# A two-pass matmul encoder layer: other offsets for the MLP's split weights, and another order of products in half of its first layer

## The chip, the cores and the metric

The kernel runs on one core of one Trainium2 chip. The metric is the device time of the program in microseconds (us); lower is better. Names of engines: PE is TensorE (PEld its weight loads), DVE is VectorE, ACT is ScalarE, POOL is GpSimd, SP is SyncE, which issues the DMAs.

## The reference, cut to what matters

One layer of an encoder over 256 tokens of width 2048, in float32: a mixer (retention and a gated delta rule), a cross-attention, a squared-ReLU MLP with hidden width 8192, and a last RMSNorm. The change touches the MLP alone:

```python
h = rms_norm(x, norm_ffn_g[l])
x = x + jnp.square(jax.nn.relu(h @ w_ff1[l])) @ w_ff2[l]
return rms_norm(x, norm_final_g)
```

`w_ff1` is 2048 by 8192 and `w_ff2` 8192 by 2048, so each holds 64 MB.

## The kernel before, in words

Every large product is made of three products of rounded parts. A float32 operand is split into a high part (rounded to the matmul type `float32r`) and a low part (the rest): high times high, high times low and low times high are added up in PSUM. The activations are held already split in tiles called `q` ("quads"): 4 blocks of 128 features, each with 256 columns of high and then 256 columns of low part.

`fetch` (L74) brings 1 MB of weights: one DMA into a tile `raw` (3 buffers), and then two halves, each split by ACT (`whi`, L92: a copy that rounds) and by DVE (`wlo`, L93: `raw` minus `whi`). `whi` and `wlo` have 3 buffers of 4096 bytes per partition each in the pool `wpipe`. `fetch` runs at a high priority of the scheduler, which orders each engine's instructions at build time by a model of their times and of what they depend on; on the chip each engine then follows its own list.

Two helpers use these halves:

- `blocks` (L155) computes 256 output features as two PSUM tiles `s0` and `s1` (b = 0 and 1). The weights are the stationary operand (128x128), the activations the moving one. For each of the 16 blocks of the inner dimension and each b it issues L171, a high product (stationary `whi`, 512 moving columns: both parts of the activations), and L172, a low product (stationary `wlo`, 256 moving columns: the high part). A call has 32 such pairs. Layer one of the MLP is 32 calls (fb = 0 to 3, b2 = 0 to 7, L936); the projections before it are made in the same way.
- `chunk` (L119) computes 512 output features with the activations stationary and the weights moving: L133 (`whi`), L134 (`wlo`) and L135 (`whi` again), 512 columns each. A call has 96 such matmuls. Layer two of the MLP is 16 calls (fb, n; L985), the last of them with `hold`, which keeps its splits in `q` tiles.

All `whi`, `wlo` and `q` tiles that MLP products read begin at a multiple of 512 bytes in a partition, and so does each slice of them: every stationary or moving operand of the MLP has offset 0 modulo 512 bytes. Three pads in the code (56 floats at L58, `PAD1`, `PAD2`) put the pools there. The delta rule's `kh` and `kl` lie at 96 modulo 512, and the retention's `vh`, `vl`, `sth` and `stl` at 288.

Ahead of the MLP stands the output projection of the cross-attention, `residual_pass` (L820) with `w_xo`. For each block of its output ACT copies half of the PSUM tile (`bo`, L176), DVE adds the other half (L177) and the residual (`rt`, L831), ACT scales and rounds it into the next `q` (L834) and squares it (L837), DVE makes the low part (L835) and adds the square to `acc2` (L838). Behind the last block PE sums `acc2` over partitions (L843). The tiles `acc2`, `sq2` and those of the attention are in the pool `xattn`, which is closed at L909. The pool `mlp` (`gfin`, `res`, `hs`) is opened behind it, at the same address. PE also transposes `rt` into `res` there (L920, 32 transposes, copied by ACT at L921).

Of the kernel before, what the change touches and what calls it, by code (L numbers as in the profile page):

```python
# [11 lines left out]
F32R = mybir.dt.float32r  # L12
# [5 lines left out]
P = 128  # L18
D = 2048
S = 256  # L20
NT = S // P
KT = D // P
# [8 lines left out]
THETA = 10000.0  # L31

PAD1, PAD2 = 8, 80
TWO_PI = 2.0 * math.pi
BIG = 1.0e30

# [13 lines left out]
def trunk(ctx: ExitStack, tc: tile.TileContext, x, mem, positions, norm_mix_g, w_in, conv_w, gdn_a_log, gdn_dt_bias,  # L50
# [4 lines left out]
    act, vec, pool, pe = nc.scalar, nc.vector, nc.gpsimd, nc.tensor  # L55
# [15 lines left out]
        return psp.tile([P, 512], F32, name="b", tag="b", bufs=4)  # L71


    def fetch(pieces, k, n, rush=False, hold=None):  # L74

        raw = wp.tile([P, k * n], F32, name="raw", tag="raw", bufs=3)
        rv = raw.rearrange("p (k n) -> p k n", k=k)
        with tc.high_priority(offset=100000):
            for off, ap in pieces:
                src = ap.rearrange("(k p) n -> p k n", p=P)  # L80
                for ks in ((slice(0, k // 2), slice(k // 2, k)) if rush else (slice(0, k),)):
                    nc.sync.dma_start(rv[:, ks, off:off + ap.shape[1]], src[:, ks, :])
            got = []
            for i in range(2):
                if hold:
                    both = hold().both
                    hi, lo = (both[:, a:a + 2, :].rearrange("p a s -> p (a s)") for a in (0, 2))
                else:
                    hi = wp.tile([P, k * n // 2], F32R, name="whi", tag="whi", bufs=3)
                    lo = wp.tile([P, k * n // 2], F32R, name="wlo", tag="wlo", bufs=3)  # L90
                src = raw[:, i * k * n // 2:(i + 1) * k * n // 2]
                act.activation(hi, src, AF.Copy)  # L92
                vec.tensor_sub(lo, src, hi.bitcast(F32))  # L93
                got.append((hi.rearrange("p (k n) -> p k n", n=n), lo.rearrange("p (k n) -> p k n", n=n)))
        return got
# [20 lines left out]
    def quad_a():  # L116
        return new_quad(hqp, 5)

    def chunk(quads, pieces_of, evac, before=None, hold=None):  # L119


        ps = stream_ps()
        parts = [(t, 0, 512, ps[t]) for t in range(NT)]
        if hold:
            parts[1:] = [(1, 0, 256, ps[1][:, :256]), (1, 256, 512, bank()[:, :256])]
        held = {q: fetch(pieces_of(q), 4, 512, hold=hold) for q in ((2, 3) if hold else ())}

        def products(q, i, part, halves):
            t, c0, c1, o = part
            xh, xl = (a[:, i, t * P:(t + 1) * P] for a in quads[q])  # L130
            wh, wl = (a[:, i % 2, c0:c1] for a in halves[i // 2])
            first, last = q == 0 and i == 0, q == 3 and i == 3
            pe.matmul(o, xh, wh, start=first, stop=False)  # L133
            pe.matmul(o, xh, wl, start=False, stop=False)  # L134
            pe.matmul(o, xl, wh, start=False, stop=last)  # L135

        for q in range(4):
            if q not in held:
                if before:
                    before(q)  # L140
                halves = fetch(pieces_of(q), 4, 512, rush=before is not None and q == 0)
# [10 lines left out]
    def cols(w, c0, n=512):  # L152
        return lambda q: [(0, w[q * 512:(q + 1) * 512, c0:c0 + n])]

    def blocks(quads, w, c0, nb, evac):  # L155

        k = 16 // nb
        ps = stream_ps()  # L160
        n = nb * P
        for g in range(KT // k):
            halves = fetch([(0, w[g * k * P:(g + 1) * k * P, c0:c0 + n])], k, n)
            for i in range(k):
                kk = g * k + i
                xh, xhl = quads[kk // 4][0][:, kk % 4, :], quads[kk // 4].both[:, kk % 4, :]
                wh, wl = halves[i // (k // 2)]
                for b in range(nb):
                    bs = slice(b * P, (b + 1) * P)
                    lh, ll = wh[:, i % (k // 2), bs], wl[:, i % (k // 2), bs]  # L170
                    pe.matmul(ps[b], lh, xhl, start=kk == 0, stop=False)  # L171
                    pe.matmul(ps[b][:, :S], ll, xh, start=False, stop=kk == KT - 1)  # L172
        for b in range(nb):
            with tc.high_priority(offset=50000):
                o = sm.tile([P, S], F32, name="bo", tag="bo", bufs=2)
                act.activation(o, ps[b][:, S:], AF.Copy)  # L176
                vec.tensor_add(o, o, ps[b][:, :S])  # L177
                evac(b, o)
# [131 lines left out]
    for k2 in range(8):  # L310
        ps = bank()
# [598 lines left out]


    fp = ctx.enter_context(tc.tile_pool(name="mlp", bufs=2))
    gfin = fp.tile([P, D], F32, name="gfin", tag="gfin", bufs=1)
    nc.sync.dma_start(gfin, norm_final_g.partition_broadcast(P))
    res = fp.tile([P, NT, D], F32, name="res", tag="res", bufs=1)
# [7 lines left out]
    for fb in range(4):  # L923
        hid = []
        for b2 in range(8):
            hs = fp.tile([P, 2, S], F32, name="hs", tag="hs", bufs=2)
            if b2 % 2 == 0:
                hid.append(quad_a())

            def evac_h(b, ps):  # L930
                vec.scalar_tensor_tensor(hs[:, b, :], ps, 0.0, ps, op0=ALU.max, op1=ALU.mult)  # L931
                qh, ql = (a[:, b2 % 2 * 2 + b, :] for a in hid[-1])
                act.activation(qh, hs[:, b, :], AF.Copy)  # L933
                vec.tensor_sub(ql, hs[:, b, :], qh.bitcast(F32))  # L934

            blocks(h3, w_ff1[0], fb * D + b2 * 256, 2, evac_h)  # L936
        for n in range(4):
            ns = slice(n * 512, (n + 1) * 512)

            def add(t, ps, c0, c1):  # L940
                got = res[:, t, n * 512 + c0:n * 512 + c1]
                vec.scalar_tensor_tensor(got, ps, rstd3q[:, t:t + 1], got, op0=ALU.mult, op1=ALU.add)  # L942
                return got

            def evac_o(t, ps, c0, c1):
                got = add(t, ps, 0, 512)
                if fb == 3:
                    square_sum(ssq4[:, t, n:n + 1], got)
                    vec.tensor_mul(got, got, gfin[:, ns])

            def evac_last(t, ps, c0, c1):
                got = add(t, ps, c0, c1)
                acc = ssq4[:, t, 4 if c0 else 3:5 if c0 else 4]
                if t == 0:
                    square_sum(acc, got)
                else:
                    junk = sm.tile([P, 512], F32, name="junk", tag="junk", bufs=1)
                    vec.scalar_tensor_tensor(junk[:, :256], got, 1.0, got, op0=ALU.mult, op1=ALU.mult, accum_out=acc)
                if not c0:
                    s = sm.tile([P, 1], F32, name="s4", tag="s4")  # L960
                    vec.tensor_reduce(s, ssq4[:, t, 0:4], axis=AX.X, op=ALU.add)
                    vec.tensor_scalar(s, s, 1.0 / D, EPS, op0=ALU.mult, op1=ALU.add)
                    sums.append(s)
                else:
                    vec.scalar_tensor_tensor(sums[t], acc, 1.0 / D, sums[t], op0=ALU.mult, op1=ALU.add)
                if c1 < 512:
                    return
                r = sm.tile([P, 1], F32, name="r4", tag="r4")
                rsqrt(r, sums[t])
                if t == 0:  # L970
# [12 lines left out]
            last = fb == 3 and n == 3  # L983
            sums = []
            chunk(hid, cols(w_ff2[0, fb * D:(fb + 1) * D, :], n * 512), evac_last if last else evac_o,  # L985
                  hold=quad_b if last else None)


_INS = ["x", "mem", "positions", "norm_mix_g", "w_in", "conv_w", "gdn_a_log", "gdn_dt_bias", "ret_gn_g", "gdn_norm_g",
# [24 lines left out]
```

## Time and profile before

| what | us |
|---|---|
| device time, median of 3 runs | 2132.74 (2132.52 to 2136.52) |
| span of the profiled execution, first to last instruction | 2135.2 |
| PE busy, share of the span | 2102.0, 98% |
| DVE busy, share | 1411.1, 66% |
| ACT busy, share | 1094.2, 51% |
| stage of the MLP in the span | about 1416 to the end |

The profile gives one time for its execution, the span; it lies 2.5 us above the median and inside the three runs. A matmul's busy time in the profile is longer than the distance to the next one, since matmuls are pipelined and their ends are modelled: what one costs in a stream is read from the distances of the starts, or from how many of them a stretch of time holds. The granted TensorE clock (PEclk) is 1.00 in the whole MLP but its last few us.

### The profile page before, as it was taken

What the parts mean: (1) busy time and instruction counts of PE and PEld (TensorE: products, weight loads), DVE (VectorE), ACT (ScalarE), POOL (GpSimd) and SP (SyncE); (2) the same over time, 40 slices, a digit from 0 to 9 for tenths busy, and PEclk for the clock granted to TensorE, in tenths of its full rate; (3) what the DMA queues carried; (4) which work ended last, traced back from release to release, by engine and by line L of the source; (5) the groups of instructions that cost most, each with busy time, mean ns of one, the idle gap of its engine ahead of it and who ended that gap; (6) DMA issues with size and microseconds to landing.
All of it is one profiled execution on the core that took longest, in us unless ns stands there. A gap on an engine that the chain in (4) does not pass through costs nothing.

```text
span 2135.2 us, 28778 instructions
## 1 busy us (share of the span) xinstructions
PE 2102.0 (98%) x11172; PEld 1800.1 (84%) x11172; DVE 1411.1 (66%) x2225; ACT 1094.2 (51%) x1700; POOL 28.5 (1%) x39
## 2 busy tenths in 40 slices
PE   8999999799999999999999999999999999999998
PEld 6878888688888889888888888888888888888887
DVE  5765779578667866786557666766556555645655
ACT  7565565354556455645455555554434434434444
POOL 0000000000000000000000000000000000000000
PEclk9999999999999999999999999999999999999999
DMA  8777656355545654555457654565566556556653
GB/s 293 249 243 241 197 183 198 96 186 194 176 144 197 202 182 144 171 199 192 156 172 256 197 187 148 178 198 180 194 197 184 192 196 185 190 197 185 189 197 138
DMA packets 316009, 405.91 MB, mean 190 GB/s; under 512 B 16592, under 2 KB 224480, under 8 KB 315744
## 3 DMA queue, kind: packets, MB, share of 16 engines
q1 hardware_dynamic: 315872, 404.08, 58.3%
q8 instruction: 87, 1.43, 0.3%
q14 instruction: 50, 0.41, 0.1%
HBM read 390.40 MB, written 13.65 MB: 189 GB/s over the span
## 4 chain that ended last, share of the span: by engine, by line
PE 93%; DMA 3%; ACT 1%; DVE 1%; SPq 1%; issue 0%; POOL 0%; ACTq 0%; POOLq 0%; DVEq 0%
PE s L171 33%; PE s L172 16%; PE s L134 13%; PE s L135 13%; PE s L133 13%; PE b L650 2%; DMA dec_d<-dec_w 1%; DMA xc<-x 1%; PE b L561 0%; DMA ct<-scr_t 0%; PE b L103 0%; DVE wlo L93 0%; PE b L104 0%; PE b L105 0%; DMA row<-crow 0%
## 5 line engine op out<-in xcount | busy, mean ns | idle before, releaser
L93 DVE TENSOR_TENSOR wlo<-raw,whi 128x1024 fp32r<-128x1024 f32 x702 | 858.4, 1224 | 521.4 <-ACT whi L92 515.4
L92 ACT ACTIVATE whi<-raw 128x1024 fp32r<-128x1024 f32 x702 | 743.9, 1061 | 727.3 <-PE s L135 377.1
L171 PE MATMUL s<-q,whi 128*128 128x512 f32 x3088 | 1080.7, 398 | 1.2 <-DVE bo L177 0.9
L172 PE MATMUL s<-q,wlo 128*128 128x256 f32 x3088 | 844.3, 281 | 5.9 <-DVE wlo L93 5.8
L171 PEld LDWEIGHTS s<-q,whi 128*128 128x128 f32 x3088 | 572.5, 188 | 126.1 <-DVE bo L177 1.2
L172 PEld LDWEIGHTS s<-q,wlo 128*128 128x128 f32 x3088 | 583.2, 189 | 20.7 <-DVE wlo L93 8.8
L134 PE MATMUL s<-wlo,q 128*128 128x512 f32 x1264 | 494.0, 391 | 0.8 <-DVE wlo L93 0.8
L135 PE MATMUL s<-whi,q 128*128 128x512 f32 x1264 | 491.3, 390 | 0.0
L133 PE MATMUL s<-whi,q 128*128 128x512 f32 x1264 | 449.5, 391 | 0.3 <-ACT whi L92 0.3
L134 PEld LDWEIGHTS s<-wlo,q 128*128 128x128 f32 x1264 | 237.8, 188 | 49.9 <-DVE wlo L93 2.0
L133 PEld LDWEIGHTS s<-whi,q 128*128 128x128 f32 x1264 | 237.3, 188 | 50.1 <-ACT whi L92 0.7
L135 PEld LDWEIGHTS s<-whi,q 128*128 128x128 f32 x1264 | 237.6, 188 | 48.2
L176 ACT ACTIVATE bo<-s 128x256 f32<-128x256 f32 x193 | 73.2, 379 | 129.5 <-PE s L172 116.8
L177 DVE TENSOR_TENSOR bo<-bo,s 128x256 f32<-128x256 f32 x193 | 80.4, 417 | 49.9 <-ACT bo L176 49.9
L516 DVE SCALAR_TENSOR_TENSOR acc<-bo,cw,acc 128x255 f32<-128x255 f32 (+2 forms) x144 | 66.1, 478 | 2.0 <-ACT acc L513 1.0
L616 DVE TENSOR_TENSOR pr<-lw,tw 32x31 f32<-32x31 f32 (+15 forms) x124 | 40.4, 325 | 9.8 <-DMA lw<-scr_l 7.7
L618 DVE TENSOR_TENSOR tw<-tw,pr 32x31 f32<-32x31 f32 (+15 forms) x124 | 40.7, 328 | 2.6
L942 DVE SCALAR_TENSOR_TENSOR res<-s,rstd3q,res 128x512 f32<-128x512 f32 (+1 forms) x32 | 22.3, 736 | 12.0 <-PE s L135 12.0
L751 ACT ACTIVATE gth<-s 128x512 f32<-128x512 f32 x32 | 19.0, 593 | 17.9 <-PE s L135 15.5
L931 DVE SCALAR_TENSOR_TENSOR hs<-bo 128x256 f32<-128x256 f32 x64 | 27.1, 423 | 1.1
L934 DVE TENSOR_TENSOR q<-hs,q 128x256 fp32r<-128x256 f32 x64 | 26.8, 419 | 0.9 <-ACT q L933 0.9
L933 ACT ACTIVATE q<-hs 128x256 fp32r<-128x256 f32 x64 | 26.2, 410 | 0.0
(292 smaller groups left out, 1084.5 us busy)
## 6 DMA issues: line engine op xcount, KB each, us to landing
raw<-w_in SPq DMA_DIRECT2D x144, 1024.0 KB, 4.9
raw<-w_ff SPq DMA_DIRECT2D x128, 1024.0 KB, 5.3
raw<-w_xkv SPq DMA_DIRECT2D x31, 1024.0 KB, 6.2
raw<-w_out SPq DMA_DIRECT2D x16, 1024.0 KB, 6.2
raw<-w_xq SPq DMA_DIRECT2D x16, 1024.0 KB, 6.1
raw<-w_xo SPq DMA_DIRECT2D x16, 1024.0 KB, 5.1
dec_d<-dec_w SPq DMA_DIRECT2D x16, 192.0 KB, 4.7
dec<-dec_d SPq DMA_DIRECT2D x8, 384.0 KB, 3.2
```

Of the source, the lines that this page charges most:

```text
L92: act.activation(hi, src, AF.Copy)
L93: vec.tensor_sub(lo, src, hi.bitcast(F32))
L133: pe.matmul(o, xh, wh, start=first, stop=False)
L134: pe.matmul(o, xh, wl, start=False, stop=False)
L135: pe.matmul(o, xl, wh, start=False, stop=last)
L171: pe.matmul(ps[b], lh, xhl, start=kk == 0, stop=False)
L172: pe.matmul(ps[b][:, :S], ll, xh, start=False, stop=kk == KT - 1)
L176: act.activation(o, ps[b][:, S:], AF.Copy)
L177: vec.tensor_add(o, o, ps[b][:, :S])
L516: vec.scalar_tensor_tensor(acc[:, d:], ps[:, :S - d], cw[:, j, blk:blk + 1], acc[:, d:], op0=ALU.mult, op1=ALU.add)
L618: vec.tensor_sub(tw[:, j + 1:32, 0:j + 1], tw[:, j + 1:32, 0:j + 1], pv)
L650: pe.matmul(pv[:, i, :], lhs(i), rhs[:, i, :], start=True, stop=True)
```

## The change

In the MLP alone the split halves of `fetch` come from a new pool, `mweights`, opened with the pool `mlp`. Its tiles, `mhi` and `mlo`, are 128 floats longer than `whi` and `wlo`, 4608 bytes, which is 9 times 512, and each begins at a multiple of 512 bytes; there are 3 buffers of each. A call uses a slice of them that begins 8 a floats into the tile, with a number `a` from 0 to 15 for the high part and 5 a modulo 16 for the low part; `a` counts the calls of a layer. So each call has its own pair of offsets, multiples of 32 bytes; within a call they stay. The first call of each layer, and call 16 of layer one, have (0, 0). The last call of layer two keeps `wpipe` and `q`, as before.

In layer one, for fb = 2 and 3 (16 of the 32 calls), the order within a block of the inner dimension becomes high b=0, high b=1, low b=0, low b=1, instead of high, low, high, low.

The pool `mweights` lies at bytes 190976 to 218624 of a partition; `xattn`, closed just ahead, had 162304 to 211560, so the two overlap. Where a new pool lies over a closed one, its first tiles wait for the last instruction that used the closed pool.

```diff
+PLACE = 128
...
-    def fetch(pieces, k, n, rush=False, hold=None):
+    def fetch(pieces, k, n, rush=False, hold=None, place=None):
...
+                elif place:
+                    own, at = place
+                    hi, lo = (own.tile([P, k * n // 2 + PLACE], F32R, name=e, tag=e, bufs=3)[:, a:a + k * n // 2]
+                              for e, a in zip(("mhi", "mlo"), at))
                 else:
...
-                for b in range(nb):
-                    bs = slice(b * P, (b + 1) * P)
-                    lh, ll = wh[:, i % (k // 2), bs], wl[:, i % (k // 2), bs]
-                    pe.matmul(ps[b], lh, xhl, start=kk == 0, stop=False)
-                    pe.matmul(ps[b][:, :S], ll, xh, start=False, stop=kk == KT - 1)
+
+                def high(b):
+                    pe.matmul(ps[b], wh[:, i % (k // 2), b * P:(b + 1) * P], xhl, start=kk == 0, stop=False)
+
+                def low(b):
+                    pe.matmul(ps[b][:, :S], wl[:, i % (k // 2), b * P:(b + 1) * P], xh, start=False, stop=kk == KT - 1)
+
+                if turns:
+                    for part in (high, low):
+                        for b in range(nb):
+                            part(b)
+                else:
+                    for b in range(nb):
+                        high(b)
+                        low(b)
...
+    mwp = ctx.enter_context(tc.tile_pool(name="mweights", bufs=3))
...
-            blocks(h3, w_ff1[0], fb * D + b2 * 256, 2, evac_h)
+            u = fb * 8 + b2
+            blocks(h3, w_ff1[0], fb * D + b2 * 256, 2, evac_h, place=(mwp, (8 * (u % 16), 8 * (5 * u % 16))), turns=fb > 1)
...
-                  hold=quad_b if last else None)
+                  hold=quad_b if last else None, place=None if last else (mwp, (8 * (4 * fb + n), 8 * (5 * (4 * fb + n) % 16))))
```

What this does to the lists of the engines: up to the end of the `w_xo` projection they stay as they were, and the differences begin there. ACT's list at that place, before, with the semaphores that an instruction waits for in brackets (`whi_13202` is the first split of `w_ff1`, `bo_13122` the copy of the last block of `w_xo`):

```order
L92 ACTIVATE whi_13202<-raw_13200 128x1024 [waits DMAHW2_49,PE_49,Activation_49]
L92 ACTIVATE whi_13206<-raw_13200 128x1024 [waits PE_49,Activation_49]
L176 ACTIVATE bo_13113<-s0_13027 128x256 [waits PE_49]
L92 ACTIVATE whi_13244<-raw_13242 128x1024 [waits DMAHW3_49,DVE_49,PE_49]
L176 ACTIVATE bo_13122<-s1_13028 128x256 [waits PE_49]
L834 ACTIVATE q_12922<-rt_10298,gains_84 128x256 [waits DVE_49]
L837 ACTIVATE sq2_13119<-rt_10298 128x256
```

ACT's list at the same place, with the change (`mhi_13205` is now the first split of `w_ff1`; L97, L191, L849 and L852 are L92, L176, L834 and L837 of before):

```order
L191 ACTIVATE bo_13113<-s0_13027 128x256 [waits PE_49]
L191 ACTIVATE bo_13122<-s1_13028 128x256 [waits PE_49]
L849 ACTIVATE q_12922<-rt_10298,gains_84 128x256 [waits DVE_49]
L852 ACTIVATE sq2_13119<-rt_10298 128x256 [waits Activation_49]
L849 ACTIVATE q_12922<-rt_10298,gains_84 128x256 [waits DVE_49]
L852 ACTIVATE sq2_13128<-rt_10298 128x256 [waits Activation_49]
L97 ACTIVATE mhi_13205<-raw_13203 128x1024 [waits DMAHW2_49,DVE_49,PE_49]
```

The first splits of the MLP stood ahead of the last work of `w_xo`; now the first stands behind all of it. The values that it waits for on DVE and PE are those of the last add to `acc2` (L838) and of the second sum over `acc2` (L843). PE's list at that place, before (`s1_13028` is the last block of `w_xo`, `s0_13198` the first of `w_ff1`):

```order
L171 MATMUL s1_13028<-q_12262,whi_13077 128x512
L172 MATMUL s1_13028<-q_12262,wlo_13078 128x256
L171 MATMUL s0_13198<-q_12295,whi_13202 128x512
L172 MATMUL s0_13198<-q_12295,wlo_13203 128x256
L171 MATMUL s1_13199<-q_12295,whi_13202 128x512
```

PE's list there with the change (L858 is the sum of L843, L936 the transposes of L920; L175 and L178 are the high and the low product):

```order
L175 MATMUL s1_13028<-q_12262,whi_13077 128x512
L178 MATMUL s1_13028<-q_12262,wlo_13078 128x256
L858 MATMUL b_13131<-ones_77,acc2_12293 128x2 x2
L936 MATMUL b_13150<-ident_76,rt_10298 128x128 x4
L936 MATMUL b_13156<-ident_76,rt_10298 128x128 x4
L936 MATMUL b_13162<-ident_76,rt_10298 128x128 x4
L936 MATMUL b_13168<-ident_76,rt_10298 128x128 x4
L175 MATMUL s0_13201<-q_12295,mhi_13205 128x512
L175 MATMUL s1_13202<-q_12295,mhi_13205 128x512
L178 MATMUL s0_13201<-q_12295,mlo_13206 128x256
```

Before, the first product of layer one followed the last of `w_xo` at once; now the sum and 16 of the 32 transposes stand between them. The other change of order is in layer one from fb = 2 on. PE's list at the start of that part, before (`s0_16507` and `s1_16508` are b = 0 and 1):

```order
L171 MATMUL s0_16507<-q_12295,whi_16511 128x512
L172 MATMUL s0_16507<-q_12295,wlo_16512 128x256
L171 MATMUL s1_16508<-q_12295,whi_16511 128x512
L172 MATMUL s1_16508<-q_12295,wlo_16512 128x256
L171 MATMUL s0_16507<-q_12295,whi_16511 128x512
```

The same place with the change:

```order
L175 MATMUL s0_16510<-q_12295,mhi_16514 128x512
L175 MATMUL s1_16511<-q_12295,mhi_16514 128x512
L178 MATMUL s0_16510<-q_12295,mlo_16515 128x256
L178 MATMUL s1_16511<-q_12295,mlo_16515 128x256
L175 MATMUL s0_16510<-q_12295,mhi_16514 128x512
```

The same five products stand there, the two high ones now ahead of the two low ones. On SP the load of `gfin` (1 MB) has moved ahead of one `w_ff1` load.

More of the change, by code (lines that the diff above doesn't have):

```diff
@@ L117, in quad_a, with chunk @@
         return new_quad(hqp, 5)
-    def chunk(quads, pieces_of, evac, before=None, hold=None):
+    def chunk(quads, pieces_of, evac, before=None, hold=None, place=None):
         ps = stream_ps()
@@ L140, in chunk @@
                     before(q)
-                halves = fetch(pieces_of(q), 4, 512, rush=before is not None and q == 0)
+                halves = fetch(pieces_of(q), 4, 512, rush=before is not None and q == 0, place=place)
                 for i in range(4):
@@ L153, in cols, with blocks @@
         return lambda q: [(0, w[q * 512:(q + 1) * 512, c0:c0 + n])]
-    def blocks(quads, w, c0, nb, evac):
+    def blocks(quads, w, c0, nb, evac, place=None, turns=False):
         k = 16 // nb
@@ L162, in blocks @@
         for g in range(KT // k):
-            halves = fetch([(0, w[g * k * P:(g + 1) * k * P, c0:c0 + n])], k, n)
+            halves = fetch([(0, w[g * k * P:(g + 1) * k * P, c0:c0 + n])], k, n, place=place)
             for i in range(k):
```

## The prediction

> **What bounds the kernel now.** I read the page first: the busy times, then the chain that ended last.
>
> ```profile
> PE 2102.0 (98%) x11172; PEld 1800.1 (84%) x11172; DVE 1411.1 (66%) x2225; ACT 1094.2 (51%) x1700; POOL 28.5 (1%) x39
> PE 93%; DMA 3%; ACT 1%; DVE 1%; SPq 1%; issue 0%; POOL 0%; ACTq 0%; POOLq 0%; DVEq 0%
> ```
>
> PE carries 93% of the chain, so time is won or lost only where PE's products get closer or further apart, or where PE stands still. Next I read two stretches inside the MLP, the first of layer two and the second of layer one.
>
> ```profile
> core 0: us, PE busy (x) PEld busy (x) DVE busy (x) ACT busy (x) POOL busy (x), PEclk, DMA share, GB/s
> 1510.00:1590.00 80.00, 80.00 (x355) 66.24 (x354) 41.75 (x42) 32.40 (x33) 0.00 (x0) 1.00 0.58 196
> 1600.00:1680.00 80.00, 80.00 (x459) 69.69 (x459) 50.27 (x70) 38.34 (x57) 0.00 (x0) 1.00 0.62 190
> ```
>
> PE is busy all 80 us at clock 1.00, DVE and ACT at most 63%. Each count holds two products begun before the stretch. So layer one starts 457 products in 80 us, 175 ns apiece, 350 ns for a pair of high and low; layer two 353, 226.6 ns apiece. No stall is left in there: in the MLP the change can act only on these two spacings, and at the seam where the MLP begins.
>
> **The seam.** This is the one part that the lists of the engines fix. PE, ACT and DVE now, at the end of `w_xo`:
>
> ```profile
> 1415.82 0.27 PE L172 MATMUL s<-q,wlo 128*128 128x256 f32 x1
> 1415.93 0.40 PE L171 MATMUL s<-q,whi 128*128 128x512 f32 x1
> ...
> 1425.36 0.50 PE L843 MATMUL b<-ones,acc 128*128 128x2 f32 x4
> ...
> 1430.12 1.91 PE L920 MATMUL b<-ident,rt 128*128 128x128 f32 x16
> ```
>
> ```profile
> 1415.79 0.39 ACT L176 ACTIVATE bo<-s 128x256 f32<-128x256 f32 x1 [1.42 <-PE s L172]
> 1416.07 1.05 ACT L92 ACTIVATE whi<-raw 128x1024 fp32r<-128x1024 f32 x1
> 1417.02 0.38 ACT L176 ACTIVATE bo<-s 128x256 f32<-128x256 f32 x1
> 1417.29 0.51 ACT L834 ACTIVATE q<-rt,gains 128x256 fp32r<-128x256 f32 x1
> 1417.69 0.41 ACT L837 ACTIVATE sq<-rt 128x256 f32<-128x256 f32 x1
> ```
>
> ```profile
> 1416.21 0.42 DVE L177 TENSOR_TENSOR bo<-bo,s 128x256 f32<-128x256 f32 x1 [0.58 <-ACT bo L176]
> 1416.67 0.42 DVE L831 TENSOR_TENSOR rt<-bo,rt 128x256 f32<-128x256 f32 x1
> 1417.16 1.23 DVE L93 TENSOR_TENSOR wlo<-raw,whi 128x1024 fp32r<-128x1024 f32 x1
> 1418.30 0.42 DVE L177 TENSOR_TENSOR bo<-bo,s 128x256 f32<-128x256 f32 x1
> 1418.63 0.48 DVE L835 SCALAR_TENSOR_TENSOR q<-rt,gains,q 128x256 fp32r<-128x256 f32 x1
> ...
> 1421.10 0.48 DVE L835 SCALAR_TENSOR_TENSOR q<-rt,gains,q 128x256 fp32r<-128x256 f32 x1
> 1421.49 0.42 DVE L838 TENSOR_TENSOR acc<-acc,sq 128x256 f32<-128x256 f32 x1
> ```
>
> Today the last low product of `w_xo` starts at 1415.82 and the first of `w_ff1` 0.11 us later, since its splits were made ahead; PE gets to the sum L843 only at 1425.36, when `acc2` has long been done. With the change no split of `w_ff1` may be written before that sum has read `acc2`, so all of it lies bare. By the rows: the last low product ends at 1416.10. ACT's second `bo` follows at 1416.1, no longer behind a 1.05 us split (today 1417.02). DVE then has two L177 and two L831; such instructions follow each other at 0.33 us (1418.30 to 1418.63), so the second L831 ends at 1417.6. ACT's two L834 and two L837 follow each other at 0.4 us (1417.29 to 1417.69), the last ending at 1418.9, and DVE's L835 and L838 (0.39 apart) end at 1419.4. PE's sum starts at 1419.45, where the next product stood at 1415.93: 3.5 us lost. The sum ends at 1419.95; the first `mhi` takes 1.05, to 1421.0, the first `mlo` 1.23 more, to 1422.3. PE meanwhile does sum and 16 transposes, work that it has today later (so no loss), to 1421.5, then two high products of 0.23, and waits about 0.4 us for `mlo`. Together **+3.9 us**, and I hold 3.0 to 4.5 possible: not below, as nothing else is on PE's list there. Queued behind the waiting split on ACT are only other splits and the copies of `res`; on DVE `rstd3q`, which waits 0.8 us for POOL inside the same hole. The load of `gfin`, now ahead of a `w_ff1` load on SP, costs nothing: three loads have landed by then, 17 us of products at 350 ns a pair, against a landing time of 5.3 us for 1 MB.
>
> A hole of that length has a second price. The trace has one like it, a wait for `wlo` early on, and the stretch that follows:
>
> ```profile
> 163.10:165.70 2.60, 0.03 (x1) 0.00 (x0) 1.61 (x3) 1.10 (x5) 0.00 (x0) 1.00 0.58 217
> ...
> 166.20:169.60 3.40, 3.40 (x13) 2.88 (x12) 1.91 (x2) 2.72 (x8) 0.00 (x0) 0.51 0.72 185
> ```
>
> After 2.6 us without products the clock was granted at 0.51 for 3.4 us, which loses 3.4 x 0.49 = 1.7 us. I take **+1.7 us**; 0 if the drop does not come or falls on the transposes alone, 3.3 for two such stretches. The Trainium skill, "TensorE: Matmul & The Clock Gate", Part 1, says the clock is set by free-running windows of 3413 ns and halves after an idle one; the 3.4 us at 0.51 agree, and by that rule a hole just over a window long either contains one or doesn't: 1.7 or nothing.
>
> **The offsets.** No row shows MLP products at another offset than 0, nor a stationary and a moving operand at different offsets. The nearest rows have both away from 0: the delta rule's `kh`, `kl` at 96 modulo 512, the retention's `vh`, `sth` at 288, beside the attention's at 0. All rows are means of one shape.
>
> ```profile
> L103 PE MATMUL b<-kth,qth 128*128 128x256 f32 x32 | 9.0, 282 | 0.0
> ...
> L561 PE MATMUL b<-kl,kh 128*128 128x512 f32 x16 | 6.3, 395 | 0.0
> ...
> L103 PE MATMUL b<-vh,sth 128*128 128x256 f32 x24 | 6.1, 281 | 0.0
> ```
>
> And layer two, at 0, from the stretch 1510 to 1590:
>
> ```profile
> L133 PE MATMUL s<-whi,q 128*128 128x512 f32 x118 | 41.2, 389 | 0.0
> ```
>
> With 256 columns offset makes no difference (281 and 282 ns). With 512 it is 395 against 389, 6 ns more. But these runs are three products long, and a layer-two run at offset 0 also starts slowly after a wait:
>
> ```profile
> 31.43 0.39 PE L135 MATMUL s<-whi,q 128*128 128x512 f32 x1
> ...
> 32.58 0.39 PE L135 MATMUL s<-whi,q 128*128 128x512 f32 x1
> ```
>
> Five products in 1.15 us there, 230 ns, before they settle at 226.6. So PE falls into step after a few products; part of the 6 ns is such a start. *Layer two:* 14 calls have new offsets, 14 x 96 = 1344 products; at 6 ns 8.1 us, at 0 nothing. High and low weights now alternate between two offsets as moving operand, which should keep PE out of step part of the time: I take half, **+4.0 us**. *Layer one:* the weights are stationary, the rest stays at 0, and slower and quicker pairs stand beside each other today already, 0.36 us (1612.73 to 1613.09, below) and 0.35. I take **0**, from the 256-column rows; the bounds are every pair at 0.36 us, 10 ns over the mean, in 30 calls of 32 pairs, +9.6 us, and the gain in the first rival.
>
> **The order.** In fb = 2 and 3, 16 calls have 16 quads of high, high, low, low, 256 in all. The list of before has such a quad here and there:
>
> ```profile
> 1612.73 0.40 PE L171 MATMUL s<-q,whi 128*128 128x512 f32 x1
> ...
> 1613.09 0.40 PE L171 MATMUL s<-q,whi 128*128 128x512 f32 x1
> ...
> 1613.44 0.63 PE L171 MATMUL s<-q,whi 128*128 128x512 f32 x2
> 1613.91 0.39 PE L172 MATMUL s<-q,wlo 128*128 128x256 f32 x2
> 1614.13 0.40 PE L171 MATMUL s<-q,whi 128*128 128x512 f32 x1
> ...
> 1614.83 0.40 PE L171 MATMUL s<-q,whi 128*128 128x512 f32 x1
> ```
>
> The quad takes 0.69 us (1613.44 to 1614.13), the two pairs behind it 0.70 (to 1614.83): at most 2.6 us over 256 quads, at the rows' rounding. I take half, **-1.3 us**, between -2.6 and +1.
>
> **The sum.** 3.9 + 1.7 + 4.0 + 0 - 1.3 = +8.3 us. On the profiled execution that gives 2135.2 + 8.3 = 2143.5; the runs' median is 2.5 lower, and the forecast is made from it: 2132.74 + 8.3 = **2141.0 us**, +0.4%. Splits as such cost nothing: the same 1024 elements per instruction on DVE and ACT, both at most 63% busy under PE.
>
> **Rivals.** *First, the other side: faster.* If stationary and moving operand at one offset are in each other's way, the 226.6 ns hold a wait that other offsets take away. For it: the 16 transposes take 1.91 us, so with some 0.27 off for the length of the last they start (1.91 - 0.27)/15 = 109 ns apart with a full weight load each, so (an estimate) 218 ns would do for 512 columns and 327 for a pair. Against: `kh` and `kl` away from 0 were not quicker. All of it would be 1344 x 9 + 960 x 23 ns = 34 us; half of it -17, with the seam and the order -13: about 2120. It wins from 2.6 ns saved per product on (8.6 us by 1344 + 1920 products; seam and order together then come to -4.3).
>
> *Second, offsets do nothing*, because PE falls into step as before: 3.9 + 1.7 - 1.3 = +4.3, 2137.0, the edge between same and slower. The Trainium skill's "SBUF — State Buffer", Who interferes with whom, says that TensorE has separate read ports for the two operands and never waits on anyone: by that rule it is this rival. The 281 and 282 ns agree, the 395 against 389 does not.
>
> *Third, every product pays.* Layer two at 6 ns (+8.1), layer one at 360 ns a pair (+9.6), with the seam's 5.6: +23.3 us, 2156. For it: a step once lost is lost for whole calls, since the offsets last a call. Against: the 256-column rows.
>
> That the change doesn't do what it says I leave out: tiles begin at multiples of 512 bytes, so the slices have the offsets named.
>
> **How the numbers follow.** Forecast (seam, part of the offset price) 0.48; first rival 0.14; second 0.22; third 0.16. A measurement can tell about 0.2%, 4.3 us, from no change. Slower by more: 0.48 + 0.16 + half of the second, 0.75; same: the other half and 0.02 of the first, 0.13; faster 0.12. The range leaves out most of the first rival and the end of the third: 2126 to 2156.
>
> **What would show it.** Right: PE idle some 3.5 us behind the last `w_xo` product, ended by DVE `acc2`, then 0.4 for `mlo`; PEclk near 0.5 for one stretch of 3.4 us there; layer two of call 0 at 226.6 ns and of the others between 227 and 232; layer one near 350 ns a pair. Wrong: no hole at the seam; or calls of layer two under 226, or pairs under 340 ns (first rival); or one call far from the rest, which would make the offset a matter of single values and the mean useless.

## The result, and the profile after

| what | before | after |
|---|---|---|
| device time, median of 4 runs, us | 2134.63 (2132.52 to 2142.83) | 2151.99 (2147.56 to 2153.41) |
| ratio, 95% interval | | 1.007 [1.0049, 1.0091] |
| span of the profiled execution, us | 2135.2 | 2151.7 |
| of it: up to the last low product of `w_xo` | 1415.8 | 1419.3 |
| from there to the third call of layer one (the seam, with all 32 transposes) | 26.49 | 33.10 |
| layer one, calls 2 to 15 / 16 to 31 | 156.81 / 179.22 | 156.71 / 178.73 |
| layer two, calls 0 to 14 / the last | 326.44 / 22.33 | 333.42 / 22.35 |

The changed kernel is slower: by 15 us (10 to 19) by the ratio, while the two medians lie 17.4 us apart. The stages are distances between starts of products in the traces. The MLP, from the last low product of `w_xo` on, took 711.3 us and takes 724.3: +13.0, namely +6.6 at the seam, +7.0 in layer two and -0.5 in the calls of layer one with the new order. The other 3.5 us of the two spans lie ahead of the seam, where both kernels run the same lists; more on them below.

The page's chain is as before, and PE is busy 15.6 us longer: PE sets the time.

```profile
PE 2117.6 (98%) x11172; PEld 1809.4 (84%) x11172; DVE 1408.1 (65%) x2225; ACT 1091.7 (51%) x1700; POOL 29.7 (1%) x39
PE 93%; DMA 3%; DVE 2%; ACT 2%; issue 1%; SPq 0%; POOL 0%; ACTq 0%; POOLq 0%; DVEq 0%
```

**The seam.** PE's timeline after: the last low product of `w_xo` (L178), the sum of `acc2` (L858), the transposes (L936) and the first products of layer one (L175 high, L178 low).

```profile
1419.29 0.27 PE L178 MATMUL s<-q,wlo 128*128 128x256 f32 x1
1422.95 1.02 PE L858 MATMUL b<-ones,acc 128*128 128x2 f32 x4 [3.39 <-DVE acc L853]
1423.83 3.65 PE L936 MATMUL b<-ident,rt 128*128 128x128 f32 x16
1427.13 1.20 PE L175 MATMUL s<-q,mhi 128*128 128x512 f32 x2
1428.13 0.63 PE L178 MATMUL s<-q,mlo 128*128 128x256 f32 x2
```

PE stands idle for 3.39 us, ended by DVE's last addition to `acc2`, where before the first product of `w_ff1` followed 0.11 us behind. Then nothing waits any more: the splits of ACT and DVE, which start only behind the sum, are covered by the transposes.

```profile
1424.00 2.95 ACT L97 ACTIVATE mhi<-raw 128x1024 fp32r<-128x1024 f32 x3 [1.68 <-PE b L858]
```

```profile
1425.09 3.50 DVE L98 TENSOR_TENSOR mlo<-raw,mhi 128x1024 fp32r<-128x1024 f32 x3
```

The transposes take 3.65 us instead of 1.91, for the clock is down. The windows of 3.4 us around the hole (PEclk is the third number from the end):

```profile
core 0: us, PE busy (x) PEld busy (x) DVE busy (x) ACT busy (x) POOL busy (x), PEclk, DMA share, GB/s
1418.90:1422.30 3.40, 0.66 (x4) 0.31 (x2) 2.39 (x7) 2.22 (x6) 0.00 (x0) 1.00 0.01 3
1422.30:1425.70 3.40, 2.75 (x13) 2.75 (x14) 1.48 (x5) 1.72 (x3) 0.70 (x1) 0.51 0.24 65
1425.70:1429.10 3.40, 3.40 (x15) 3.11 (x14) 2.89 (x3) 3.20 (x6) 0.00 (x0) 0.50 0.72 272
1429.10:1432.50 3.40, 3.40 (x24) 3.05 (x23) 0.39 (x1) 1.48 (x2) 0.00 (x0) 0.99 0.91 278
```

The clock is halved for 6.8 us: behind a window in which PE was busy 0.66 of 3.40 us, and again behind one with 2.75; behind a window that is full it is back. Half of 6.8 us is 3.4, and 3.39 + 3.4 is the 6.6 of the table to 0.2 us.

**Layer two.** The first product of the calls 0 to 3 (L138, which was L133), and the first of the layer-one call behind them:

```profile
1519.55 0.40 PE L138 MATMUL s<-mhi,q 128*128 128x512 f32 x1
...
1541.34 0.63 PE L138 MATMUL s<-mhi,q 128*128 128x512 f32 x2
...
1563.70 0.39 PE L138 MATMUL s<-mhi,q 128*128 128x512 f32 x1
...
1585.69 0.39 PE L138 MATMUL s<-mhi,q 128*128 128x512 f32 x1
...
1608.14 0.63 PE L175 MATMUL s<-q,mhi 128*128 128x512 f32 x2
```

The calls take 21.79, 22.36, 21.99 and 22.45 us; by 96 products that is 227.0, 232.9, 229.1 and 233.9 ns each. Call 0, with its parts at (0, 0), is as before; the others are dearer, each by its own amount, with no idle time of PE in them. Over the 15 calls in order, from unrounded starts: 226.9, 232.9, 229.0, 233.8, 232.4, 231.1, 233.4, 232.9, then 227.0, 232.9, 229.0, 233.8, 233.3, 231.1, 233.4. The list repeats after 8 calls, 256 bytes, and call 8, at (256, 256), is as cheap as call 0. Calls 4 and 12 alone differ, by 0.9 ns, and I have no reason for it.

**Layer one.** A pair of high and low took 349.8 to 351.0 ns before; now it takes 347.2 to 352.8 by call in the old order, 345.5 to 353.0 in the new one. The mean stays.

**Ahead of the seam.** The same lists, and yet 3.5 us. The stretch of the mixer where PE has waits, before and after:

```profile
400.00:420.00 20.00, 13.18 (x94) 11.34 (x93) 6.12 (x21) 5.14 (x20) 2.02 (x2) 0.97 0.06 14
```

```profile
400.00:420.00 20.00, 15.62 (x75) 13.95 (x76) 3.72 (x13) 4.55 (x19) 1.01 (x1) 0.61 0.04 14
```

The granted clock was 0.97 there in one execution and 0.61 in the other. Of eight further traces whose lists ahead of the MLP are those of before (below), the last low product of `w_xo` starts anywhere from 1410.8 to 1422.1 us. So the 3.5 us between two executions can't be put down to the change, and the times of single runs, which scatter from 2133 to 2144 us for the kernel before (one slow execution of 2317 us, at a clock of 0.85, is left out), tell little. The experiments are read by the distances in the MLP, and where the whole time counts, by 11 or 12 runs against 17 to 23 of the kernel before: the two medians, and a ratio with its 95% interval, which is not the quotient of these medians.

### The profile page after: what moved, and what is told of

Same layout as the page of the kernel before. It is cut to its first block, busy times and chain, and to the rows that moved or that the text cites. A ratio compares the mean times of both kernels' runs of the same rounds, so it can differ in the third digit from the quotient of the medians.

```text
span 2151.7 us, 28775 instructions
## 1 busy us (share of the span) xinstructions
PE 2117.6 (98%) x11172; PEld 1809.4 (84%) x11172; DVE 1408.1 (65%) x2225; ACT 1091.7 (51%) x1700; POOL 29.7 (1%) x39
## 4 chain that ended last, share of the span: by engine, by line
PE 93%; DMA 3%; DVE 2%; ACT 2%; issue 1%; SPq 0%; POOL 0%; ACTq 0%; POOLq 0%; DVEq 0%
PE s L175 32%; PE s L178 16%; PE s L139 13%; PE s L138 13%; PE s L140 13%; PE b L665 2%; DMA row<-crow 1%; DVE wlo L98 1%; DMA dec_d<-dec_w 1%; ACT whi L97 1%; PE b L576 0%; PE b L108 0%; PE b L109 0%; PE b L110 0%; DMA ct<-scr_t 0%
## 5 line engine op out<-in xcount | busy, mean ns | idle before, releaser
L175 PE MATMUL s<-q,whi 128*128 128x512 f32 x2064 | 724.8, 398 | 1.2 <-DVE bo L192 0.9
L98 DVE TENSOR_TENSOR wlo<-raw,whi 128x1024 fp32r<-128x1024 f32 x454 | 554.3, 1222 | 257.3 <-ACT whi L97 254.1
L97 ACT ACTIVATE whi<-raw 128x1024 fp32r<-128x1024 f32 x454 | 479.7, 1058 | 398.5 <-PE s L140 192.7
L178 PE MATMUL s<-q,wlo 128*128 128x256 f32 x2064 | 564.7, 282 | 4.7 <-DVE wlo L98 4.6
L98 DVE TENSOR_TENSOR mlo<-raw,mhi 128x1024 fp32r<-128x1024 f32 x248 | 303.7, 1225 | 285.5 <-ACT mhi L97 284.4
L175 PEld LDWEIGHTS s<-q,whi 128*128 128x128 f32 x2064 | 382.8, 189 | 83.8 <-DVE bo L192 1.2
L97 ACT ACTIVATE mhi<-raw 128x1024 fp32r<-128x1024 f32 x248 | 262.8, 1060 | 359.1 <-PE s L140 187.1
L178 PEld LDWEIGHTS s<-q,wlo 128*128 128x128 f32 x2064 | 390.2, 189 | 16.2 <-DVE wlo L98 7.6
L175 PE MATMUL s<-q,mhi 128*128 128x512 f32 x1024 | 339.1, 395 | 0.0
L140 PE MATMUL s<-whi,q 128*128 128x512 f32 x784 | 304.6, 390 | 0.0
L138 PE MATMUL s<-whi,q 128*128 128x512 f32 x784 | 281.5, 391 | 0.0
L178 PE MATMUL s<-q,mlo 128*128 128x256 f32 x1024 | 242.5, 280 | 0.0
L178 PEld LDWEIGHTS s<-q,mlo 128*128 128x128 f32 x1024 | 192.7, 188 | 24.3
L175 PEld LDWEIGHTS s<-q,mhi 128*128 128x128 f32 x1024 | 173.5, 188 | 21.0
L140 PE MATMUL s<-mhi,q 128*128 128x512 f32 x480 | 189.1, 394 | 0.0
L138 PEld LDWEIGHTS s<-whi,q 128*128 128x128 f32 x784 | 147.4, 188 | 30.7 <-ACT q L246 0.4
L138 PE MATMUL s<-mhi,q 128*128 128x512 f32 x480 | 170.2, 394 | 0.0
L191 ACT ACTIVATE bo<-s 128x256 f32<-128x256 f32 x193 | 71.1, 377 | 111.1 <-PE s L178 98.4
```

The lines of the kernel that those rows point to most:

```text
L175: pe.matmul(ps[b], wh[:, i % (k // 2), b * P:(b + 1) * P], xhl, start=kk == 0, stop=False)
L178: pe.matmul(ps[b][:, :S], wl[:, i % (k // 2), b * P:(b + 1) * P], xh, start=False, stop=kk == KT - 1)
```

## The experiments

The diffs show only the lines or arguments that change. My theory: two prices that add, the seam (pool) and the offsets in layer two, the second from operands out of step. Rivals: that one of the two carries all; for the offsets, that it is the alternation of high and low (the prediction's reason), the distance between the two operands, or the position of one by itself.

**The pool alone.** The new pool for all calls, every offset 0, old order:

```diff
-  place=(mwp, (8 * (u % 16), 8 * (5 * u % 16))), turns=fb > 1)
+  place=(mwp, (0, 0)))
-  place=None if last else (mwp, (8 * (4 * fb + n), 8 * (5 * (4 * fb + n) % 16))))
+  place=None if last else (mwp, (0, 0)))
```

> The new pool with every offset at (0, 0) and the old order: the change without its offsets and its turns. Theory (the seam is a price by itself, paid to the pool): the stretch from the last low product of w_xo to the start of the third call of layer one takes 33 us as in the changed kernel, against 26.5 before; layer two stays at 226.7 ns a product, layer one at 350 ns a pair; the time is 5 to 8 us over before. Rival (the cost of layer two comes from the new tiles, their place or length, and not from the offsets): layer two at 230 ns or more here too, the time 12 us or more over before.

Measured: 2141.59 against 2135.48 us, ratio 1.0023 [1.0011, 1.0035], which is +4.9 us (the medians: +6.1). Layer two 226.7 ns, layer one 350 as before, the MLP 716.6 us, +5.3, all at the seam (31.83 us, where I expected 33). PE's timeline and the windows there:

```profile
1414.43 0.27 PE L178 MATMUL s<-q,wlo 128*128 128x256 f32 x1
1418.10 0.83 PE L858 MATMUL b<-ones,acc 128*128 128x2 f32 x4 [3.39 <-DVE acc L853]
1418.79 3.38 PE L936 MATMUL b<-ident,rt 128*128 128x128 f32 x16
```

```profile
1414.90:1418.30 3.40, 0.20 (x2) 0.20 (x2) 2.90 (x8) 1.75 (x5) 0.00 (x0) 1.00 0.02 6
1418.30:1421.70 3.40, 3.40 (x18) 3.40 (x18) 1.92 (x4) 2.74 (x3) 0.70 (x1) 0.50 0.53 164
1421.70:1425.10 3.40, 3.40 (x22) 2.99 (x21) 1.85 (x2) 2.35 (x6) 0.00 (x0) 0.99 0.74 244
```

The same hole of 3.39 us, but it fell so that the window behind it is full of work, and the clock is down for 3.4 us, not 6.8. What the hole cost in these two traces, 5.3 or 6.6 us, thus goes with where it fell among the windows. The Trainium skill, "TensorE: Matmul & The Clock Gate", Part 1, has free-running windows of 3413 ns; the two traces agree, with 3.4 and 6.8 us of half clock. But the window behind which the clock fell need not be empty: PE was busy for 0.20 us of it here and for 0.66 after the change.

**The change without the seam.** Call 0 of layer one keeps the old pool, so its splits are made ahead again:

```diff
-  place=(mwp, (8 * (u % 16), 8 * (5 * u % 16))), turns=fb > 1)
+  place=(mwp, (8 * (u % 16), 8 * (5 * u % 16))) if u else None, turns=fb > 1)
```

> The change, but call 0 of layer one takes its splits from the old pool; its offsets were (0, 0) anyway. Theory: the first splits no longer wait for the closed pool, the stretch at the seam is back at 26 to 27.5 us, with no stretch of halved clock there; layer two stays at 231.5 ns a product; the time is 6 to 8 us over before. Rival (the hole only moves to call 1, whose splits wait for the same pool): the stretch stays over 30 us and the time 13 us or more over before.

Measured: 2145.31 against 2135.48, ratio 1.0038 [1.0024, 1.0053], which is +8.1 us (the medians: +9.8); the MLP 717.6, +6.3, with layer two call by call as after the change. PE is busy through the whole seam at full clock:

```profile
1416.30:1443.00 26.70, 26.70 (x168) 23.72 (x167) 15.07 (x24) 15.77 (x28) 0.70 (x1) 1.00 0.64 197
```

In the traces the two parts come to 5.3 + 6.3 = 11.6 us of the MLP's 13.0; what is left is the seam, 5.3 here and 6.6 there. By the ratios they come to 4.9 + 8.1 = 13.0 us against 15. Within these intervals they add.

**High and low at one offset.** Both parts at 32 bytes times the call, seam taken out as above:

```diff
+  place=(mwp, (8 * (u % 16), 8 * (u % 16))) if u else None, turns=fb > 1)
+  place=None if last else (mwp, (8 * (4 * fb + n), 8 * (4 * fb + n))))
```

> As without the seam, but high and low weights of a call have the same offset, 32 bytes times the number of the call (layer two 0 to 14, layer one 0 to 15 in the old order and 0 to 15 again in the new). Theory (each product whose moving operand begins off a multiple of 256 bytes pays for itself): calls 0 and 8 of layer two at 226.7 to 227 ns a product, the others at 229 to 234. Rival (the prediction's: PE falls out of step because high and low weights alternate between two offsets): all calls of layer two at 226.7 to 227. Layer one: pairs of calls 256 bytes apart give the same time by the first, 347 to 353 ns a pair.

The first products of layer two's calls 0 to 3, and the next call:

```profile
1504.47 0.40 PE L138 MATMUL s<-mhi,q 128*128 128x512 f32 x1
...
1526.24 0.40 PE L138 MATMUL s<-mhi,q 128*128 128x512 f32 x1
...
1548.64 0.40 PE L138 MATMUL s<-mhi,q 128*128 128x512 f32 x1
...
1570.63 0.40 PE L138 MATMUL s<-mhi,q 128*128 128x512 f32 x1
...
1593.04 0.39 PE L175 MATMUL s<-q,mhi 128*128 128x512 f32 x1
```

21.77, 22.40, 21.99 and 22.41 us: 226.8, 233.3, 229.1 and 233.4 ns. Without any alternation the calls cost as much as with it, so alternation is not needed to make them dear. (2138.91 us, one run.)

**The other operand.** The kernel before, its weights at 0, but layer two's activations (the stationary operand, four tiles a call) in a pool of their own at 32 bytes times (4 fb + tile):

```diff
+    def placed_quad(pl, a):
+        flat = pl.tile([P, 8 * S + 128], F32R, name="pq", tag="pq", bufs=4)[:, a:a + 8 * S]
...
-                hid.append(quad_a())
+                hid.append(placed_quad(hidp, 8 * (4 * fb + b2 // 2)))
```

> The kernel before, but the four activation tiles of layer two, its stationary operand, are laid at 32 bytes times (4 fb + number of the tile); the weights stay at offset 0. Theory A (the moving operand's own position decides): every tile's products at 226.7 ns. Theory B (the distance between the stationary and the moving operand decides, since PE reads both at once): tiles 0 and 8 of the 16 at 226.7, the others at 229 to 234, as in the changed kernel. The time is that of before by A, 5 to 8 us more by B.

Call 5 reads tiles at 128, 160, 192 and 224 bytes, 24 products each. The first product of each, and of the next call:

```profile
1710.19 0.64 PE L140 MATMUL s<-whi,pq 128*128 128x512 f32 x2
...
1715.78 0.63 PE L140 MATMUL s<-whi,pq 128*128 128x512 f32 x2
...
1721.38 0.63 PE L140 MATMUL s<-whi,pq 128*128 128x512 f32 x2
...
1726.89 0.63 PE L140 MATMUL s<-whi,pq 128*128 128x512 f32 x2
...
1732.49 0.64 PE L140 MATMUL s<-whi,pq 128*128 128x512 f32 x2
```

5.59, 5.60, 5.51 and 5.60 us, that is 232.9, 233.3, 229.6 and 233.3 ns. In calls 0 to 3 the tile at 64 bytes took 233.4 ns. So moving the stationary operand costs the same, and the cheap place mirrors: activations at 192 bytes are like weights at 64 (229.1 above). What counts is moving minus stationary address, modulo 256. Tiles 0 and 8, at distance 0, I expected at 226.7 ns; they took 227.4 to 228.6, each next to tiles that are off their place. (2144.46 us, one run.)

**Everything moved together.** The kernel before with its first pad at 96 floats, not 56: all operands at 160 modulo 512, distance 0.

```diff
-    cp.tile([P, 56], F32, name="pad0")
+    cp.tile([P, 96], F32, name="pad0")
```

> The kernel before with its first pad 40 floats longer, so that every weight and activation tile of the large products lies at 160 modulo 512 bytes instead of 0; their distances stay 0. Theory (the distance between the moving and the stationary operand modulo 256 bytes decides): layer two at 226.7 ns a product, layer one at 350 ns a pair, as before. Rival (an operand off a multiple of 256 bytes pays by its own position, whichever of the two it is): layer two at 232 to 236 ns.

Calls 0 and 1 of layer two:

```profile
1508.67 0.40 PE L133 MATMUL s<-whi,q 128*128 128x512 f32 x1
...
1530.44 0.61 PE L133 MATMUL s<-whi,q 128*128 128x512 f32 x2
```

21.77 us, 226.8 ns, and the MLP 711.3 us, as before. At this position, 160 bytes, position by itself costs nothing; the third reading falls. (2136.18 us, one run.)

**Finer steps.** Both parts of layer two at 0, 1, 2, 4, 8 and more floats, layer one at 0 in the old order, no hole at the seam:

```diff
+  place=None if last else (mwp, ((0, 1, 2, 4, 8, 12, 16, 20, 24, 28, 32, 40, 48, 56, 60)[4 * fb + n],) * 2))
```

> As without the seam, layer two with both offsets alike at 0, 1, 2, 4, 8, 12, 16, 20, 24, 28, 32, 40, 48, 56, 60 floats in calls 0 to 14, layer one at 0 in the old order. Theory (lines of 64 bytes, four of them to a period of 256): 226.7 ns at 0 and 229 at 16 floats, 232 to 234 at 8 and 24 to 56 as in the steps of 8 measured so far, and a small step off a line (1, 2, 4 floats) costs nearly as much as 8 floats, 230 to 234. Rival (only the size of the overlap counts): the price grows evenly from 0 floats to 8, about 1 ns at 1 float and 3 at 4.

Calls 0 to 3 (0, 4, 8 and 16 bytes) and the next call:

```profile
1509.87 0.40 PE L138 MATMUL s<-mhi,q 128*128 128x512 f32 x1
...
1531.64 0.40 PE L138 MATMUL s<-mhi,q 128*128 128x512 f32 x1
...
1554.47 0.39 PE L138 MATMUL s<-mhi,q 128*128 128x512 f32 x1
...
1576.96 0.39 PE L138 MATMUL s<-mhi,q 128*128 128x512 f32 x1
...
1599.20 0.39 PE L175 MATMUL s<-q,mhi 128*128 128x512 f32 x1
```

By the call in ns, worked out in the same way from all 15:

| bytes | 0 | 4 | 8 | 16 | 32 | 48 | 64 | 80 | 96 | 112 | 128 | 160 | 192 | 224 | 240 |
|---|---|---|---|---|---|---|---|---|---|---|---|---|---|---|---|
| ns | 226.8 | 237.8 | 234.3 | 231.7 | 233.4 | 233.2 | 228.9 | 231.2 | 233.4 | 231.1 | 232.4 | 234.2 | 233.4 | 233.3 | 233.3 |

One float off is the dearest of all. Nothing grows with the distance: 0 is free, 64 bytes pays 2 ns, and all else 4 to 11. My own theory had small steps at 230 to 234 ns and missed that one. (2145.41 us, one run.)

**The high weights alone, the low weights alone.** The part not moved stays at distance 0, seam taken out. These ask whether each product pays for itself:

```diff
+  place=None if last else (mwp, (8 * (4 * fb + n), 0)))
...
+  place=None if last else (mwp, (0, 8 * (4 * fb + n))))
```

> As without the seam, but only the high weights have offsets, 32 bytes times the number of the call; low weights at 0. Two of three products of layer two move. Theory (each product pays its own price): calls of layer two at 226.7 plus two thirds of the price that equal offsets cost, 231.2 in call 1, 228.2 in call 2, 231.2 in call 3, 230.5 in call 4, 231.7 in call 5, each within 0.7 ns. Rival (the price is of the whole sequence, a step lost once is lost for all three products): the full price as with equal offsets, or none.

Measured in calls 1 to 5: 232.1, 232.7, 232.2, 230.4 and 232.3 ns. Adding by product fits calls 4 and 5, misses calls 1 and 3 by 1 ns and call 2 by 4.5. The full price of equal offsets (233.4, 229.0, 233.4, 232.3, 234.2) misses all five by 1.2 to 3.7. So the run with the low weights alone, one product of three, where the two readings lie further apart:

> Layer two's low weights alone lie 32 bytes x call from the activations; the two high products of each three stay at distance 0. Layer one's calls have their low weights moved likewise, and call 0 of layer one keeps the old pool. Own-distance theory (each product pays by its own distance, with the prices of the run in which both parts moved): 228.9, 227.5, 228.9, 228.6 and 229.2 ns in calls 1 to 5, +-0.7. Sequence theory (a product at distance 0 pays too, once it follows one that is not): the two unmoved products pay most of it, so 230 to 234 in calls 1, 3, 4 and 5, and above 228.2 in call 2. Both: 226.7 in calls 0 and 8, the seam as in the kernel before (26.5 us), time 2136 to 2142.

The calls 0 to 3 and the next call, low weights alone:

```profile
1515.42 0.40 PE L138 MATMUL s<-mhi,q 128*128 128x512 f32 x1
...
1537.23 0.62 PE L138 MATMUL s<-mhi,q 128*128 128x512 f32 x2
...
1559.48 0.62 PE L138 MATMUL s<-mhi,q 128*128 128x512 f32 x2
...
1581.84 0.62 PE L138 MATMUL s<-mhi,q 128*128 128x512 f32 x2
...
1604.10 0.63 PE L175 MATMUL s<-q,mhi 128*128 128x512 f32 x2
```

227.2, 231.8, 232.9 and 231.9 ns, then 230.9 and 232.8 in calls 4 and 5. That is the sequence reading: one product of three off its place makes the whole stream pay, 5.3 ns a product over the 13 moved calls, against 6.0 with all three moved to one offset. The starts show it product by product: from a product of the low activations to the next high product, neither of them moved, it is 230.9 ns on average in these calls, and 226.9 in calls 1 to 3 of the kernel before. And alternation has a price of its own after all: in call 2, 0 and 64 bytes mixed take 232.9 and 232.7 ns in the two runs, where 0 alone takes 226.7 and 64 alone 229.0. Only with distance 0 for every product of the stream did it run at 226.7 ns. (2141.28 and 2149.18 us, one run each.)

**The order alone.** All calls of the helper `blocks`, the projections too, in the order high, high, low, low; nothing else:

```diff
                 for b in range(nb):
-                    bs = slice(b * P, (b + 1) * P)
-                    lh, ll = wh[:, i % (k // 2), bs], wl[:, i % (k // 2), bs]
-                    pe.matmul(ps[b], lh, xhl, start=kk == 0, stop=False)
-                    pe.matmul(ps[b][:, :S], ll, xh, start=False, stop=kk == KT - 1)
+                    pe.matmul(ps[b], wh[:, i % (k // 2), b * P:(b + 1) * P], xhl, start=kk == 0, stop=False)
+                for b in range(nb):
+                    pe.matmul(ps[b][:, :S], wl[:, i % (k // 2), b * P:(b + 1) * P], xh, start=False, stop=kk == KT - 1)
```

> The kernel before with both high products ahead of both low ones in every call of that helper, offsets as before. Theory (the order by itself is worth 1.5 ns a pair, by the changed kernel's turned calls at offset 0, 348.2 to 348.6 ns against 350): layer one at 348 to 349 ns a pair, the whole kernel 3 to 5 us under before, 0.1 to 0.2%. Rival (the order does nothing but change the step in which PE runs): layer one at 350 and the time within 2 us of before.

Missed: 2140.40 against 2135.76, ratio 1.0017 [1.0005, 1.0029], slower. In layer one a pair takes 348.3 ns instead of 350, and the MLP is 1.8 us shorter, as expected; but the medians differ by +4.6, so some 6 us are lost ahead of the MLP. One wait in the mixer has that size: PE's for `t`, which DVE makes once a DMA has brought `ct`. PE and DVE there, before:

```profile
392.81 2.05 PE L643 MATMUL b<-alt,t 128*128 128x128 f32 x16 [1.10 <-DVE t L633]
392.01 0.45 DVE L625 STREAM_TRANSPOSE cu<-ct 128x256 f32<-128x256 f32 x1 [0.82 <-DMA ct<-scr_t]
```

With the new order:

```profile
396.19 3.48 PE L642 MATMUL b<-alt,t 128*128 128x128 f32 x16 [7.05 <-DVE t L632]
395.38 0.45 DVE L624 STREAM_TRANSPOSE cu<-ct 128x256 f32<-128x256 f32 x1 [4.12 <-DMA ct<-scr_t]
```

PE waits 7.05 us instead of 1.10, and DVE 4.12 us for the DMA instead of 0.82. In the next run, with the same order, PE waits 6.43 us; in each of the ten other traces, which keep the old order there, 0.80 to 1.41. The clock falls behind it too: over 380 to 400 us it is 0.83 instead of 1.00. Why PE comes to that wait earlier and the DMA lands later I have not isolated.

**Order and distance in layer one.** The same order, and the second pad at 96 floats, which puts the activation tiles of the cross-attention and of layer one at 64 modulo 256:

```diff
-PAD1, PAD2 = 8, 80
+PAD1, PAD2 = 8, 96
```

> The order as above, and the pad ahead of the activation tiles of the cross-attention and of layer one 16 floats longer: these, as the moving operand, lie 64 bytes behind a multiple of 256, the weights at 0; in the survey with equal offsets the turned calls at that distance (weights at 192) took 345.5 ns a pair. Theory (distance decides, whichever operand is moved): layer one at 345 to 346 ns a pair, 4.6 us less than before, the w_xq calls 1 us less, the rest as by the order alone: 6 to 9 us under before, 0.3 to 0.4%. Rival (it was the weights' own place): layer one at 348 to 351, the time as by the order alone.

Half missed: 2135.18 against 2135.76, ratio 0.9994 [0.9982, 1.0007], where I expected 6 to 9 us less. A pair takes 345.0 ns and the MLP 706.4 us, -4.9; the wait in the mixer, here too, eats that. Then the same in the MLP alone: the order `turns=True` in layer one only, the pad, no new pool.

> The kernel before with the new order in layer one alone, and the pad ahead of the activation tiles of the cross-attention and of layer one 16 floats longer; no new pool, layer two as before. Theory: from the last low product of w_xo to the last product 706 to 707 us instead of 711.3, layer one at 345.0 ns a pair, layer two at 226.7, nothing changed ahead of the attention: 4 to 6 us under before, 0.2 to 0.3%. Rival (what the order lost in the mixer was not the order but the longer pad or a shift of the clock's windows): no gain in the whole time, within 2 us of before.

Two neighbouring calls of layer one:

```profile
1788.23 0.62 PE L175 MATMUL s<-q,whi 128*128 128x512 f32 x2
...
1799.27 0.39 PE L175 MATMUL s<-q,whi 128*128 128x512 f32 x1
```

11.04 us by 32 pairs, 345.0 ns; the MLP 706.3, -5.0. 2130.77 against 2135.13 us, ratio 0.9973 [0.996, 0.9986]: faster than both kernels, and 4 to 6 us under the one before. PE's wait for `t` is 0.85 us in it, so what the two runs above lost there goes with the order and not with the pad.

## Why the prediction was right, and where it was off

*The seam, +5.6 forecast.* Right, place, releaser and size: 3.39 us idle ended by DVE, where I had 3.5, and the clock drop behind it. On the clock my row was right (a fall behind 2.6 us without products) and the rule that I quoted was not: the hole is shorter than a window of 3413 ns, so it can't hold a whole one, and by "contains one or doesn't" there would have been no fall. My 0.4 us for `mlo` did not come, since the transposes, at half clock, last longer than the splits. The drop lasted 3.4 us in the pool-alone run, as I took it, and 6.8 in the profile after: 5.3 and 6.6 us in all. The pool alone costs 4.9 us by the ratio.

*Layer two, +4.0.* Right in sign, mis-sized: 7.0 us, a mean price of 5.2 ns on 1344 products where I took 3. The step that failed is halving the 6 ns, first as a start that fades, and then as alternation. The price lasts the whole call, and it is there with no alternation at all (233.3 ns). That the 6 ns came out near the truth is luck: `kl` and `kh` both lie at 96 modulo 512, distance 0, where the runs show no price, and their row is still 395 ns with everything moved by 160 bytes. So no row behind the forecast was about a distance, the 256-column rows included. What I called being out of step is real in one way: an unmoved product pays when its neighbour is moved, and 0 and 64 bytes mixed are dearer than either alone. The range of 227 to 232 ns for the calls was too low; but for call 8, again at distance 0, they lie at 229.0 to 233.8.

*Layer one, 0.* Right on average, -0.1 us over calls 2 to 15. It is not indifference, though: calls move by -2.8 and +2.8 ns a pair and cancel, which no row of mine foresaw; so the 0 is luck. In that the first rival had a grain: at the right distance a pair does get quicker, 345.0 ns with the new order, call after call. It never got near the 327 ns I reckoned for it, an estimate whose step from 128 columns to 512 no row bears out.

*The order, -1.3.* Right in sign: -0.5 in the turned calls. Alone it is 1.7 ns a pair, 0.9 us over 512 pairs; their offsets took back the rest.

*The sum.* +8.3 forecast, +13.0 measured in the MLP; 3.0 of the difference is layer two and 1.0 the seam. By the ratio it is 15 (10 to 19); what lies above 13 is not told from the scatter.

*The rivals.* Faster: no call of layer two came under 226 ns. Offsets do nothing: falls, layer two +7.0 us with the seam taken out. Its rule, in the Trainium skill's "SBUF — State Buffer", Who interferes with whom, that TensorE's two read ports are independent, doesn't hold for the time here: 226.8 against 233.3 ns with only the distance of the operands changed. Every product pays: nearly so in layer two (7.0 of 8.1), not in layer one.

Open: why distance 0, and in part 64 bytes, suits a stream of these products, and what PE does in the lost 5 ns. The traces show the spacing and no cause. Also open is why PE's wait for `t` in the mixer grows when the order is changed there.

## What to carry to other kernels

Where PE is the bound, look at the addresses of both operands modulo 256, not at either alone: in a stream of 512-column products with a new stationary operand each, one part off its place raised 226.7 ns to 232. Lay tiles out so that all products of a stream agree, and try the distance for each shape of stream by itself, since layer one was quickest at 64 bytes and layer two at 0. And before opening a pool over a closed one on the path, let the first tiles come from a pool that is already there: that alone was 5 us here.

## What the runs showed of the hardware

- The price of a distance repeats every 256 bytes, to 0.9 ns, is signed (weights at 64 bytes 229.1 ns, activations at 64 bytes 233.4), and is highest at 4 bytes (237.8) of the 15 distances tried.
- The order high, high, low, low is quicker than high, low, high, low by 1.7 ns a pair at distance 0 (348.3 against 350).
- A stream of three products pays as a whole: with one of the three off its place, products that were not moved also start 231 ns apart instead of 227.
- An idle stretch of 3.4 us cost 1.9 or 3.2 us more through the clock, by where it fell: behind a window of 3.4 us that PE filled the clock was back, behind one with 2.75 us busy it stayed at half.
